# A four-mixer encoder on one core: split weights kept in device memory for a layer's second half, low parts on VectorE, and another clock for the order of emission

## The chip, the cores and the metric

The kernel runs on 1 core of one Trainium2 chip, as one program. The metric is the time of an execution on the device in microseconds (us); less is better. Below, PE is TensorE's matmul, PEld its weight load, DVE is VectorE, ACT ScalarE, POOL GpSimd and SP SyncE; L365 is line 365 of the kernel's file.

## The reference

Input `x` is (1, 1024, 1024) float32: 1024 tokens of 1024 features. Two layers; each normalises its input, projects it once, runs four causal mixers on pieces of the projection, gates and merges them, and adds an output projection. A last normalisation follows.

```python
def _layer(x, norm_w, w_in, ..., w_branch, w_out):
    h = _rmsnorm(x, norm_w)
    p = h @ w_in                                  # 1024 -> 11408 columns
    ...
    u_a = _rwkv7_branch(rw_r, rw_k, rw_v, ...)    # each u is (tokens, 512)
    u_b = _retention_branch(rt_q, rt_k, rt_v, rt_z, ret_norm_w)
    u_c = _ssd_branch(sd_xbc, sd_z, sd_dt, ...)
    u_d = _gdn_branch(gd_qkv, gd_z, gd_b, gd_a, ...)
    gates = jax.nn.sigmoid(gate_logits.reshape(b, s, N_BRANCH, D_MODEL))
    merged = gates[:, :, 0] * (u_a @ w_branch[0])
    ...
    return x + merged @ w_out
```

RWKV-7 and gated DeltaNet are recurrences which the kernel writes chunk by chunk, with the inverse of a unit lower triangular matrix for each chunk and head.

## The kernel before, in words

**Passes.** The 1024 tokens are two halves of 512. A pass is one half of one layer; there are four: layer 0 first half, layer 0 second half, layer 1 first half, layer 1 second half. In the trace they take about 940 us each. A pass has 228 slabs of weights, of 128 x 512 float32 (256 KB); with the output projections of a pass running in the next, all four read 912. The two halves of a layer read the same weights.

**Slabs.** A product takes weights and activations each as a high part H (a cast to the type fp32r) and a low part L = value − H, and sums H·H, H·L and L·H: a slab costs 12 matmuls of 128x512. `prefetch(g)`, when the products get to slab g, has SP load slabs up to g + 5 into `raw` (three buffers), has H made of slabs up to g + 3 (ACT, now and then DVE) and L of those up to g + 2 (`low`, which calls `subtract`), both into `hl` (four buffers). `subtract` is also what makes the L parts of the mixers' outputs (`u`), of the normalised input (`hL`) and of operands inside the units (`w`, `GE`, `GF`). It takes POOL or DVE, by the clock described next.

**What sets the order.** Each engine runs its instructions in the order in which the program was written, so the program's writer matters: `mixers` runs a list of tasks (the steps of 12 units for each pass: 2 retention, 4 DeltaNet, 2 SSD, 4 RWKV-7) and the stream of products, written in `FIRST` and `PLAN`. Whenever a task's next step should be ready by the `Clock`, it is emitted; otherwise a few matmuls of the product stream are. `Clock` is an estimate kept while the program is written: a time for each engine, the last write and read of every 128 elements of a tile, a cost for each kind of instruction, and 0.2 us from engine to engine. `sooner(a, b, n)` asks it which of two engines would be done first. It ends up in no instruction, only in their order.

**Inside a unit.** `inverse` works on `invw`: some twenty small DVE steps on 4 to 128 elements, with small matmuls (`m`) of PE between them. `ev_conv` makes a causal convolution with three DVE instructions on `cvy`. `rsqrt` has POOL take a power into `rs`. SP's queue holds, in the order of writing, the loads of `raw`, the loads of `rope` (two tiles `tg` and `cvy` for each q and k of retention, four pairs a pass), and loads of the next pass's input in `norm`; ACT's queue has the stores of the layer's output and some loads.

Of the kernel before, what the change touches and what calls it, by code (L numbers as in the profile page):

```python
# [16 lines left out]
P = 128  # L17
D = 1024
S = 1024
T = 512          # tokens per pass  # L20
NC = 4           # chunks per pass
C = 128          # tokens per chunk
# [5 lines left out]
# units in the order in which a pass runs them  # L28
# [3 lines left out]
# what a unit takes from the input projection, in the order of the products, with its place in memory; what has two  # L32
# places is 256 columns wide and has the tokens in the partitions
# [11 lines left out]
# The products of a pass in the order in which the tensor engine takes them, between the steps of the units.  # L45
# "out" is the output projection of the pass before, "norm" the normalisation of the input of the next pass;
# the last branch is merged in two steps, gates and projections.
# [4 lines left out]
# the first pass  # L52
# [10 lines left out]
# the others  # L63
# [36 lines left out]
def slabs_of(it):  # L100
    """The slabs of weights of an item of the plan, each of four blocks of 128 rows and 128 columns, or of two of
    128 rows and 256 columns."""
# [16 lines left out]
def sequence(npass):  # L119
    """The items of the plan for all passes, each with its pass."""  # L120
    seq = [(p - (it[0] == "out"), it) for p in range(npass) for it in (PLAN if p else FIRST)]
    return [x for x in seq if x != (npass - 1, ("norm",))] + [(npass - 1, it) for it in PLAN if it[0] == "out"]
# [30 lines left out]
# columns of the packed small parameters  # L153
# [10 lines left out]
def ssd_blk(idx, role):  # L164
    """Index of a 128-wide block of xbc."""
# [46 lines left out]
# constants: name -> (first column, width)  # L212
# [10 lines left out]
def make_consts():  # L223
# [42 lines left out]
    rope = np.stack([ct, st, ct * sc, st * sc])          # 4, P, S  # L266
# [4 lines left out]
class Clock:  # L271
    """An estimate, in microseconds, of when the engines get to what is emitted; it orders the steps."""
    HAND = 0.2       # from one engine to another

    def __init__(self):
        self.t = {e: 0.0 for e in ("pe", "vector", "scalar", "gpsimd", "dma")}
        self.slot, self.owner, self.written, self.read = {}, {}, {}, {}
        self.step = 0.0

    def place(self, tile, key):  # L280
        """The tile lies where the last one with this key lay."""
# [3 lines left out]
    def grains(self, ap):  # L285
        """Pieces of 128 elements of a tile's place which an operand touches; a bank of PSUM counts as one, as its
        users take turns."""
# [12 lines left out]
    def op(self, eng, outs, ins, cost):  # L300
        at = self.t[eng]
        gi, go = [g for a in ins for g in self.grains(a)], [g for a in outs for g in self.grains(a)]
        for g in gi:
            w = self.written.get(g)
            if w:
                at = max(at, w[0] + (0.13 if w[1] == eng else self.HAND))
        for g in go + [g for g in gi if g[1] < 0]:
            for d in (self.written, self.read):
                w = d.get(g)
                if w and w[1] != eng:  # L310
                    at = max(at, w[0] + self.HAND)
        end = self.wait(eng, at) + cost
        for g in gi:
# [10 lines left out]
    def settled(self, *aps):  # L324
        """When the last writes to these operands are over."""
# [6 lines left out]
    def cost(self, eng, name, n):  # L332
        if eng == "vector":
            return 0.07 + n * (0.52e-3 if name == "copy" else 1.04e-3)
        if eng == "scalar":
            return 0.1 + n * 0.83e-3
        return {"memset": 0.1 + n * 0.83e-3, "tensor_copy": 0.2 + n * 3.4e-3, "affine_select": 0.2 + n * 0.85e-3,
                "pow": 0.4 + n * 0.165}.get(name, 0.2 + n * 1.97e-3)


class Engine:
    """An engine whose instructions the clock sees."""
# [4 lines left out]
    def __getattr__(self, what):  # L347
        fn = getattr(self.real, what)

        def call(*a, **k):  # L350
# [8 lines left out]
            else:  # L359
                nm = "pow" if ALU.pow in a else what  # L360
                if what == "tensor_copy" and self.name == "vector" and not any(x.tensor.name.split("_")[0] in "mgy" for x in ops):
                    nm = "copy"
                self.clock.op(self.name, outs, [x for x in ops if not any(x is o for o in outs)],
                              self.clock.cost(self.name, nm, n))
# [11 lines left out]
def finish(gen):  # L376
    """What the generator returns, after all its steps."""
# [12 lines left out]
class Trunk:  # L390
# [12 lines left out]
    # ---------------------------------------------------------------- tiles  # L403
# [29 lines left out]
    # ---------------------------------------------------------------- tensor engine, with its time kept  # L433
    def mm(self, out, lhsT, rhs, **k):
        n, m = (int(np.prod(ap.shape[1:])) for ap in (rhs, lhsT))
        cost = (2 if m > 64 else 1.2) * max(n, m, 16) * 0.84e-3 if rhs.dtype == F32 else max(n, 64) * 0.42e-3
# [1574 lines left out]
```

## Time and profile before

| | |
|---|---|
| median of 3 runs | 3782.73 us (3778.8 to 3783.42) |
| profiled execution, span from first to last instruction | 3775.2 us, 7.5 us below that median; the profile gives no other time of that execution |
| granted TensorE clock | 0.978 |
| busy: PE / DVE / ACT / POOL | 3577.6 / 2543.6 / 1401.4 / 1790.6 us |
| HBM read / written | 280.69 / 10.49 MB |
| loads of `raw` | 912, 256.0 KB each |

A page's matmuls are pipelined and their ends modelled: the busy time of PE counts more than its issue. In lists of groups the columns are: line, engine, operation, out<-in with shapes, count | busy us, mean ns of one | idle time before them and who ended it. In lists of waits: who waits for whom, us in total, times, longest. In windows: stretch, length, then busy us and count for PE, PEld, DVE, ACT, POOL, then granted clock, share of the DMA engines and GB/s.

### The profile page before, as it was taken

What the parts mean: (1) busy time and instruction counts of PE and PEld (TensorE: products, weight loads), DVE (VectorE), ACT (ScalarE), POOL (GpSimd) and SP (SyncE); (2) the same over time, 40 slices, a digit from 0 to 9 for tenths busy, and PEclk for the clock granted to TensorE, in tenths of its full rate; (3) what the DMA queues carried; (4) which work ended last, traced back from release to release, by engine and by line L of the source; (5) the groups of instructions that cost most, each with busy time, mean ns of one, the idle gap of its engine ahead of it and who ended that gap; (6) DMA issues with size and microseconds to landing.
All of it is one profiled execution on the core that took longest, in us unless ns stands there. A gap on an engine that the chain in (4) does not pass through costs nothing. (4 is left out here: it accounts for less than half of the span.)

```text
span 3775.2 us, 66152 instructions
## 1 busy us (share of the span) xinstructions
PE 3577.6 (95%) x24904; PEld 2864.7 (76%) x24904; DVE 2543.6 (67%) x5607; ACT 1401.4 (37%) x3121; POOL 1790.6 (47%) x1846
## 2 busy tenths in 40 slices
PE   7999999999999999999999999999999999999998
PEld 5777877777877787777787778777778778867777
DVE  6678666766577856567657775757665876675664
ACT  4433343333243334333324334433332433443333
POOL 4534554545453445445545445444454534454444
PEclk9999999999999999999999999999999999999999
DMA  3212222113322222212332222221243222221124
GB/s 121 72 59 65 73 72 61 52 60 114 124 76 79 65 73 68 61 54 71 113 126 75 71 73 70 62 64 55 71 125 113 86 64 68 70 65 58 57 76 148
DMA packets 162176, 295.48 MB, mean 78 GB/s; under 512 B 17984, under 2 KB 21440, under 8 KB 161856
## 3 DMA queue, kind: packets, MB, share of 16 engines
q1 hardware_dynamic: 150192, 271.22, 24.1%
q10 hardware_dynamic: 11664, 20.02, 1.6%
q8 instruction: 197, 3.23, 0.4%
q14 instruction: 123, 1.01, 0.1%
HBM read 280.69 MB, written 10.49 MB: 77 GB/s over the span
## 5 line engine op out<-in xcount | busy, mean ns | idle before, releaser
L438 PE MATMUL g<-hH,hl 128*128 128x512 f32 (+1 forms) x5176 | 1773.9, 415 | 8.4 <-DVE cvraw L365 4.9
L365 POOL TENSOR_TENSOR hl<-raw,hl 128x512 fp32r<-128x512 f32 x700 | 960.6, 1377 | 745.0 <-ACT hl L365 659.2
L438 PEld LDWEIGHTS g<-hH,hl 128*128 128x128 f32 (+1 forms) x5176 | 974.9, 191 | 240.5 <-issue 10.3
L438 PE MATMUL g<-hL,hl 128*128 128x512 f32 x2600 | 1040.8, 400 | 0.0
L365 ACT CAST hl<-raw 128x512 fp32r<-128x512 f32 x851 | 521.8, 618 | 684.4 <-PE g L438 270.0
L438 PE MATMUL g<-u,hl 128*128 128x512 f32 (+1 forms) x2112 | 608.9, 411 | 24.1 <-ACT hH L365 9.7
L438 PEld LDWEIGHTS g<-hL,hl 128*128 128x128 f32 x2600 | 496.8, 191 | 113.0 <-issue 8.6
L438 PEld LDWEIGHTS g<-u,hl 128*128 128x128 f32 (+1 forms) x2112 | 391.5, 191 | 122.3 <-ACT hH L365 12.2
L365 POOL TENSOR_TENSOR rs<-rs,mhalf 128x4 f32<-128x4 f32 (+2 forms) x80 | 106.5, 1331 | 401.5 <-DVE rs L365 401.2
L365 DVE SCALAR_TENSOR_TENSOR cvy<-cvraw,par,cvy 128x512 f32<-128x512 f32 x244 | 257.7, 1056 | 41.8 <-ACT cvy L365 30.4
L365 DVE TENSOR_TENSOR hl<-raw,hl 128x512 fp32r<-128x512 f32 x212 | 211.5, 1007 | 27.4 <-ACT hl L365 26.3
L438 PE MATMUL g<-hl,hH 128*128 128x256 f32 x1024 | 190.0, 285 | 2.7 <-DVE hl L365 2.7
L365 DVE TENSOR_TENSOR invw<-invw 128x4 f32<-128x4 f32 (+3 forms) x464 | 164.3, 354 | 15.9
L365 ACT COPY cvraw<-g 128x512 f32<-128x512 f32 (+1 forms) x160 | 93.5, 585 | 187.5 <-PE g L438 145.6
L438 PEld LDWEIGHTS g<-hl,hH 128*128 128x128 f32 x1024 | 160.3, 191 | 3.6 <-DVE hl L365 2.9
L365 POOL TENSOR_SCALAR_AFFINE_SELECT GA<-GA 128x512 f32<-128x512 f32 x128 | 85.2, 672 | 121.8 <-ACT GA L365 121.8
L365 ACT ACTIVATE cvraw<-cvy 128x512 f32<-128x512 f32 x80 | 50.2, 628 | 234.9 <-DVE cvy L365 217.2
L365 POOL TENSOR_TENSOR acc<-acc,tg 128x512 f32<-128x512 f32 x64 | 90.3, 1411 | 81.4 <-DVE tg L365 70.6
L438 PE MATMUL g<-hl,hL 128*128 128x256 f32 x512 | 125.6, 283 | 0.0
L438 PE MATMUL m<-w,w 64*128 64x256 f32 (+1 forms) x640 | 115.5, 312 | 1.3 <-ACT w L365 0.5
L365 ACT ACTIVATE tg<-g 128x512 f32<-128x512 f32 x100 | 59.6, 596 | 150.1 <-PE g L438 109.1
L365 ACT ACTIVATE in<-g 128x512 f32<-128x512 f32 x84 | 49.3, 597 | 169.2 <-PE g L438 169.2
(340 smaller groups left out, 5682.2 us busy)
## 6 DMA issues: line engine op xcount, KB each, us to landing
raw<-W SPq DMA_DIRECT2D x912, 256.0 KB, 2.6
w<-x ACTq DMA_DIRECT2D x32, 256.0 KB, 3.5
tg<-rope SPq DMA_DIRECT2D x16, 256.0 KB, 3.0
cvy<-rope SPq DMA_DIRECT2D x16, 256.0 KB, 3.4
w<-x SPq DMA_DIRECT2D x16, 256.0 KB, 4.4
x<-tg ACTq DMA_DIRECT2D x12, 256.0 KB, 2.1
x<-cvy ACTq DMA_DIRECT2D x12, 256.0 KB, 2.0
GA<-xT SPq DMA_DIRECT2D x8, 256.0 KB, 5.1
```

Of the source, the lines that this page charges most:

```text
L365: return fn(*a, **k)
L438: self.nc.tensor.matmul(out, lhsT, rhs, **k)
```

## The change

Three things change.

**Kept weights.** In a layer's first half (passes of even number) `low` now also stores the finished `hl` tile, H and L together (512 KB), into a tile of device memory, on SP's queue. In the second half no `raw` slab is loaded and nothing is split: `load_slab` loads `hl` from that tile. Such a load is not issued ahead of what `split` was asked for, that is g + 3 in place of g + 5.

**Low parts.** `subtract` always takes DVE.

**Clock.** It has a port that DVE and POOL share: an instruction that `ported` names starts when the port is free and holds it. Several costs are other numbers, matmuls' among them. This changes the order of what is emitted, and what `sooner` answers. Comments went away too.

```diff
 class Clock:
     HAND = 0.2
+    SAME = 0.13
...
+        self.port = 0.0
...
-    def op(self, eng, outs, ins, cost):
+    def op(self, eng, outs, ins, cost, port=False):
...
+        if port:
+            at = max(at, self.port)
         end = self.wait(eng, at) + cost
+        if port:
+            self.port = end
...
-        return {"memset": 0.1 + n * 0.83e-3, "tensor_copy": 0.2 + n * 3.4e-3, "affine_select": 0.2 + n * 0.85e-3,
-                "pow": 0.4 + n * 0.165}.get(name, 0.2 + n * 1.97e-3)
+        return {"memset": 0.1 + n * 0.83e-3, "tensor_copy": 0.13 + n * 1e-3, "affine_select": 0.1 + n * 0.95e-3,
+                "pow": 0.4 + n * 0.15}.get(name, 0.2 + n * 1.97e-3)
+
+    def ported(self, eng, name, ins):
+        if eng == "scalar" or not ins or any(self.slot.get(x.tensor.name, ("",))[0] in ("m", "g", "y") for x in ins):
+            return False
+        return eng == "gpsimd" or name in ("tensor_tensor", "scalar_tensor_tensor", "tensor_copy", "copy") \
+            or (name == "tensor_scalar" and int(np.prod(ins[0].shape[1:])) >= 32)
+
+    def free(self, eng, port=False):
+        return max(self.t[eng], self.port) if port else self.t[eng]
...
-        cost = (2 if m > 64 else 1.2) * max(n, m, 16) * 0.84e-3 if rhs.dtype == F32 else max(n, 64) * 0.42e-3
+        if rhs.dtype != F32:
+            cost = max(n, 128) * 0.456e-3
+        elif m <= 64:
+            cost = 0.03 if m <= 32 else 0.11 if n <= 64 else n * 1.7e-3
+        else:
+            cost = 2 * max(n, m) * 0.85e-3
...
     def split(self, high, low):
         nc = self.nc
+        self.high = high
         flat = lambda ap: ap.rearrange("p k c -> p (k c)")
         for i in range(self.next_low, low + 1):
-            if i in self.hl:
+            if i in self.raw and i in self.hl:
                 self.low(i)
         for i in range(self.slab_next_split, high + 1):
             self.load_slab(i)
+            if self.kept(i):
+                self.slab_next_split = i + 1
+                continue
...
+        p, sl = self.slabs[i]
+        w = self.wsplit[p // NHALF, sl] = self.dr.tile([P, 8 * P], F32, tag=f"ws{i}", name=f"ws{i}")
+        self.nc.sync.dma_start(w, hl.rearrange("p a k c -> p (a k c)").bitcast(F32))
         self.next_low = i + 1
...
     def sooner(self, a, b, n, what=""):
         ck = self.ck
-        return ck.t[a] + ck.cost(a, what, n) <= ck.t[b] + ck.cost(b, what, n) + 0.8
+        at = {e: ck.free(e, e != "scalar") + ck.cost(e, what, n) for e in (a, b)}
+        return at[a] <= at[b] + 0.8

     def subtract(self, out, a, b):
-        e = self.nc.gpsimd if self.sooner("gpsimd", "vector", int(np.prod(out.shape[1:]))) else self.nc.vector
+        e = self.nc.vector
         e.tensor_tensor(out, a, b, ALU.subtract)

     def load_slab(self, i):
         while self.slab_next_dma <= i:
-            r = self.t([P, 4 * P], "raw", bufs=3)
-            self.nc.sync.dma_start(r, self.slab_ap(self.slab_next_dma))
-            self.raw[self.slab_next_dma] = r
+            n = self.slab_next_dma
+            if self.kept(n):
+                if n > self.high:
+                    break
+                p, sl = self.slabs[n]
+                hl = self.t([P, 2, 4, P], "hl", bufs=4, dt=F32R)
+                self.nc.sync.dma_start(hl.rearrange("p a k c -> p (a k c)").bitcast(F32), self.wsplit.pop((p // NHALF, sl)))
+                self.hl[n] = hl
+            else:
+                r = self.t([P, 4 * P], "raw", bufs=3)
+                self.nc.sync.dma_start(r, self.slab_ap(n))
+                self.raw[n] = r
             self.slab_next_dma += 1
+
+    def kept(self, i):
+        return self.slabs[i][0] % NHALF == 1
```

Counted over the whole program: SP's loads of `raw` go from 912 to 456, and 456 stores `ws<-hl` and 456 loads `hl<-ws` join them. POOL's subtractions of slabs go from 700 to 0 and its other subtractions of low parts, 154 of 256 columns and 87 of 512, to 0, DVE's of slabs from 212 to 456; casts of slabs go from 851 to 443 on ACT and from 61 to 13 on DVE. PE has 19362 instructions in both.

SP's queue at the program's start, before (`ws` below is a store into device memory, `raw` a slab's load):

```order
L365 DMA raw_85<-W 128x512
L365 DMA up_87<-up 128x256
L365 DMA raw_159<-W 128x512
L365 DMA raw_163<-W 128x512
L365 DMA raw_165<-W 128x512
L365 DMA raw_178<-W 128x512
```

and with the change:

```order
L387 DMA raw_85<-W 128x512
L387 DMA up_87<-up 128x256
L387 DMA ws_115<-hl_111 128x1024
L387 DMA ws_132<-hl_128 128x1024
L387 DMA ws_163<-hl_160 128x1024
L387 DMA raw_165<-W 128x512
L387 DMA raw_169<-W 128x512
L387 DMA raw_171<-W 128x512
L387 DMA ws_182<-hl_167 128x1024
```

The fourth slab's load, `raw_159` before and `raw_165` now, stands behind the stores of the first three. Further on in a first half stores and loads alternate.

SP's queue where the second pass begins, with the loads for retention's q and k, before:

```order
L365 DMA raw_9159<-W 128x512
L365 DMA raw_9182<-W 128x512
L365 DMA tg_9201<-rope 128x512
L365 DMA cvy_9202<-rope 128x512
L365 DMA raw_9209<-W 128x512
L365 DMA raw_9226<-W 128x512
L365 DMA tg_9247<-rope 128x512
```

and with the change:

```order
L387 DMA ws_9529<-hl_9507 128x1024
L387 DMA ws_9552<-hl_9531 128x1024
L387 DMA hl_9554<-ws_163 128x1024
L387 DMA hl_9574<-ws_182 128x1024
L387 DMA hl_9594<-ws_203 128x1024
L387 DMA tg_9613<-rope 128x512
L387 DMA cvy_9614<-rope 128x512
L387 DMA hl_9618<-ws_241 128x1024
L387 DMA hl_9632<-ws_295 128x1024
L387 DMA tg_9653<-rope 128x512
```

The first kept slabs come right behind the last stores, and the two `rope` loads stand among loads of `hl` where they stood among loads of `raw`.

DVE's queue in the third pass, at the start of the inverse of an RWKV-7 unit that the prediction shows at 2529.88 us (`invw` is the inverse's work tile, `GR` what its first small matmuls take, `hl<-raw` a slab's low part), before:

```order
L365 SCALAR_TENSOR_TENSOR GD_22_24801<-in_36_23388,par_17647,w_31_24006 128x2x128
L365 TENSOR_TENSOR GD_22_24801<-in_36_23448,w_31_24006 128x2x128
L365 TENSOR_TENSOR GF_31_24808<-w_43_24228,GF_31_24808 128x256
L365 TENSOR_TENSOR GE_31_24807<-GD_22_24801,w_59_24806 128x512
L365 TENSOR_TENSOR invw_16_24817<-GA_23_24651,con_81 32x128 x4
L365 TENSOR_REDUCE invw_16_24817<-invw_16_24817 128x32
L365 TENSOR_TENSOR GR_22_24652<-invw_16_24817,con_81 128x64
L365 TENSOR_TENSOR GR_22_24652<-invw_16_24817,con_81 128x32
L365 TENSOR_TENSOR GR_22_24652<-invw_16_24817,con_81 128x16
L365 COPY invw_16_24817<-con_81 128x32
L365 TENSOR_SCALAR sh_24827<-strw_1_92,em_24014 128x128
L365 TENSOR_TENSOR invw_16_24817<-m_24868,invw_16_24817 128x4
```

and with the change:

```order
L387 TENSOR_TENSOR hl_24816<-raw_24725,hl_24816 128x512
L387 SCALAR_TENSOR_TENSOR GD_22_24891<-in_36_23390,par_17491,w_31_24115 128x2x128
L387 TENSOR_TENSOR GD_22_24891<-in_36_23456,w_31_24115 128x2x128
L387 TENSOR_TENSOR w_63_24894<-w_53_24282,w_63_24894 128x256
L387 TENSOR_TENSOR w_50_24895<-w_39_24287,w_50_24895 128x256
L387 TENSOR_TENSOR GF_31_24898<-w_43_24289,GF_31_24898 128x256
L387 TENSOR_TENSOR GE_31_24897<-GD_22_24891,w_59_24896 128x512
L387 TENSOR_TENSOR invw_16_24907<-GA_23_24735,con_81 32x128 x4
L387 TENSOR_REDUCE invw_16_24907<-invw_16_24907 128x32
L387 TENSOR_TENSOR GR_22_24736<-invw_16_24907,con_81 128x64
L387 TENSOR_TENSOR GR_22_24736<-invw_16_24907,con_81 128x32
L387 TENSOR_TENSOR GR_22_24736<-invw_16_24907,con_81 128x16
```

DVE now has a slab's low part and two of the unit's (`w`) ahead of the inverse's first steps; the steps themselves stand in the same order. Three rows further on another slab's low part, `hl_24877<-raw_24770`, comes ahead of the inverse's next step.

More of the change, by code (lines that the diff above doesn't have):

```diff
@@ L305, in op @@
             if w:
-                at = max(at, w[0] + (0.13 if w[1] == eng else self.HAND))
+                at = max(at, w[0] + (self.SAME if w[1] == eng else self.HAND))
         for g in go + [g for g in gi if g[1] < 0]:
@@ L362, in call @@
                     nm = "copy"
-                self.clock.op(self.name, outs, [x for x in ops if not any(x is o for o in outs)],
-                              self.clock.cost(self.name, nm, n))
+                ins = [x for x in ops if not any(x is o for o in outs)]
+                c, port = self.clock.cost(self.name, nm, n), self.clock.ported(self.name, what, ins)
+                if port and what == "scalar_tensor_tensor":
+                    c += n * 0.12e-3
+                if self.name == "scalar" and k.get("accum_out") is not None:
+                    c += 0.15
+                self.clock.op(self.name, outs, ins, c, port)
             return fn(*a, **k)
@@ L440, in tr @@
     def tr(self, out, in_, ident):
-        self.ck.op("pe", [out], [in_], max(out.shape[-1], in_.shape[-1]) * 0.84e-3)
+        self.ck.op("pe", [out], [in_], max(out.shape[-1], in_.shape[-1]) * 0.86e-3)
         self.nc.tensor.transpose(out, in_, ident)
@@ L453, in setup @@
         self.slab_pos = 0
+        self.wsplit = {}
         self.units_done = 0
```

## The prediction

> **What bounds the kernel now.** I read the page first, then who TensorE waits for, then one of those waits in the timeline, then the DMA share of the stretches where TensorE runs densest.
>
> ```profile
> span 3775.2 us, 66152 instructions
> PE 3577.6 (95%) x24904; PEld 2864.7 (76%) x24904; DVE 2543.6 (67%) x5607; ACT 1401.4 (37%) x3121; POOL 1790.6 (47%) x1846
> ```
>
> PE is the bound: 95% busy, 197.6 us idle (3775.2 − 3577.6). No other engine is near full, so a change can win only what PE waits, plus what its modelled ends hide. The chain that ended last shows how much they hide: in the last dense stretch 324 products take 75.27 us, 0.232 us each, while the page gives the same kind 0.414 us.
>
> ```profile
> 3685.14 75.27 PE g L438 x324
> L438 PE MATMUL g<-hH,hl 128*128 128x512 f32 x5152 | 1762.0, 414 | 8.4 <-DVE cvraw L365 4.9 <-DVE hl L365 2.0 <-POOL hl L365 1.3
> ```
>
> So a wait seen as idle time is about 0.18 us (0.414 − 0.232) longer than it shows. Whom PE waits for:
>
> ```profile
> PE m L438 <- DVE invw L365: 77.3, 62, 2.7
> PE m L438 <- DVE GR L365: 13.8, 10, 3.6
> PE m L438 <- DVE GE L365: 12.9, 18, 1.5
> PE m L438 <- DVE stgdn L365: 11.0, 14, 1.9
> ...
> PE m L438 <- DVE b L365: 0.2, 1, 0.2
> ```
>
> These are the first four and the last of 16 rows that name DVE; together they are 161.2 us in 149 waits. With 149 × 0.18 = 27 us hidden, PE loses about **188 us** to DVE. All other releasers (ACT hH, ACT u, POOL hl and so on) are about 24 us. Why DVE is late is seen at one of the longest waits, in the third pass, at 2531 us (start, length, engine, instruction):
>
> ```profile
> 2528.18 1.77 DVE L365 TENSOR_TENSOR GE<-GD,w 128x512 fp32r<-128x512 f32 x1
> 2529.37 1.72 POOL L365 TENSOR_TENSOR hl<-raw,hl 128x512 fp32r<-128x512 f32 x1
> 2529.88 2.61 DVE L365 TENSOR_TENSOR invw<-GA,con 32x128 f32<-32x128 f32 x4
> 2532.94 1.48 DVE L365 TENSOR_TENSOR GR<-invw,con 128x64 f32<-128x64 f32 x3
> 2534.56 0.74 PE L438 MATMUL m<-GR,con 128*128 128x112 f32 x2 [2.68 <-DVE invw L365]
> ...
> L365 DVE TENSOR_TENSOR invw<-GA,con x128: 268/289/1362, 562.5 to 3636.5; 32x128 f32<-32x128 f32 x128
> L365 DVE TENSOR_TENSOR invw<-invw x464: 166/168/1349, 198.4 to 3644.8; 128x4 f32<-128x4 f32 x87, 128x8 f32<-128x8 f32 x41, 128x16 f32<-128x16 f32 x23, 128x32 f32<-128x32 f32 x4
> L365 DVE TENSOR_TENSOR hl<-raw,hl x212: 655/698/1790, 20.3 to 3718.8; 128x512 fp32r<-128x512 f32 x106
> ```
>
> The last three rows give min/median/max in ns. Four small products of `invw` take 2.61 us, though one takes 0.289 in the median (1.16 for four); they begin while POOL subtracts a low part until 2531.09, and the next such row stretches too. DVE instructions that read two SBUF tiles stop while POOL works, up to about 1.3 us each. That lateness, 1.45 us here alone, is most of PE's 2.68.
>
> **The change, part by part.** *POOL's low parts go to DVE.* The order counts 700 subtractions of slabs less on POOL, 154 of 256 columns and 87 of 512.
>
> ```profile
> L365 POOL TENSOR_TENSOR hl<-raw,hl 128x512 fp32r<-128x512 f32 x700 | 960.6, 1377 | 745.0 <-ACT hl L365 659.2 <-DVE hl L365 52.7 <-PE m L438 16.6
> L365 POOL TENSOR_TENSOR w<-w,w 128x256 fp32r<-128x256 f32 x56 | 46.4, 847 | 21.1 <-ACT w L365 21.1
> L365 POOL TENSOR_TENSOR u<-yC,u 128x512 fp32r<-128x512 f32 x30 | 44.0, 1466 | 16.9 <-ACT u L365 16.9
> ```
>
> POOL loses 960.6 + 154 × 0.847 + 87 × 1.466 = 1219 us of 1790.6, that is 68%; 572 us stay. I take PE's waits on DVE to shrink in the same proportion, since what makes DVE late is being stopped by POOL: 188 × 0.68 = **−128 us**. Bounds: nothing gained (DVE late for its own queue's sake), and all 188.
>
> *What DVE gets.* Slab subtractions go from 212 to 456: 244 × 0.698 = 170 us. The 154 narrow ones, at an estimated 0.40 (a little over half of 0.698), are 62, the 87 wide ones 61. Casts fall from 61 to 13:
>
> ```profile
> L365 DVE CAST hl<-raw 128x512 fp32r<-128x512 f32 x61 | 40.3, 661 | 75.9 <-PE g L438 58.1 <-DMA raw<-W 14.2 <-POOL hl L365 3.5
> L365 DVE SCALAR_TENSOR_TENSOR cvy<-cvraw,par,cvy 128x512 f32<-128x512 f32 x244 | 257.7, 1056 | 41.8 <-ACT cvy L365 30.4
> L365 DVE SCALAR_TENSOR_TENSOR cvy<-cvraw,par,cvy x244: 750/752/1710, 138.0 to 3243.6; 128x512 f32<-128x512 f32 x122
> L365 DVE TENSOR_TENSOR hl<-raw,hl 128x512 fp32r<-128x512 f32 x212 | 211.5, 1007 | 27.4 <-ACT hl L365 26.3
> L365 DVE TENSOR_TENSOR invw<-invw 128x4 f32<-128x4 f32 (+3 forms) x464 | 164.3, 354 | 15.9
> ```
>
> 48 × 0.661 = 32 less, so +261 gross. What comes back is mean less median: 244 × 0.304 for `cvy`, 212 × 0.309 for `hl`, 464 × 0.186 for `invw`: 226 us in three groups, of which 68% is 154, and the groups below them give more. DVE ends near 2543.6 + 261 − 154 = 2650, at most 70% of the span. I cost this at nothing: PE's products hide it, and in the second halves DVE loses its slab work altogether. If that cover is gone, the price is the slower rival below.
>
> *ACT* loses 408 casts (851 to 443), 250 us of an engine that is 37% busy: nothing.
>
> *The stores and the double loads.* 456 raw loads stay, 456 stores and 456 loads of 512 KB join, all on SP's queue. In a first half each slab then moves 768 KB (786 kB) where it moved 256; the two halves differ only there.
>
> ```profile
> 975.00:1000.00 25.00, 25.00 (x156) 22.11 (x155) 11.22 (x21) 7.50 (x13) 11.42 (x9) 1.00 0.46 141
> 3685.00:3760.00 75.00, 75.00 (x325) 60.57 (x324) 39.24 (x52) 27.69 (x46) 32.55 (x24) 1.00 0.48 155
> raw<-W SPq DMA_DIRECT2D x912, 256.0 KB, 2.6
> x<-tg ACTq DMA_DIRECT2D x12, 256.0 KB, 2.1
> SPq L365 <- DVE in L365: 36.8, 12, 8.1
> ```
>
> The last two columns of the windows are the share of the DMA engines and GB/s: a full share would carry 141/0.46 = 307 to 155/0.48 = 323 GB/s. A slab of 12 products takes PE 12 × 0.232 = 2.79 us at its densest, the 786 kB 2.43 to 2.56. It fits, barely; a store of 256 KB lands in 2.1 us, no slower than a load. Value 0; upper bound, should stores and loads mixed run a fifth slower: 3.2 us, 0.4 us a slab over the (496 + 540)/12 = 86 slabs of the two 100 us stretches around the ends of the first halves, **+35**.
>
> ```profile
> 900.00:1000.00 100.00, 96.51 (x496) 79.70 (x495) 63.69 (x89) 36.71 (x63) 55.79 (x38) 0.98 0.43 132
> 2800.00:2900.00 100.00, 99.89 (x540) 82.31 (x539) 56.64 (x109) 30.64 (x59) 43.15 (x31) 1.00 0.42 132
> ```
>
> The Trainium skill (SBUF — State Buffer, the summary of rules for kernel authors) counts 358 GB/s between HBM and SBUF, which would make a slab 2.2 us; the trace's share implies less, and I keep the trace's. By either figure the term is zero.
>
> In a second half a slab's load takes the place of the slab four before it, so it is issued when PE ends that one, three slabs (8.4 us) ahead of its use. It lands in an estimated 2.6 + 0.85 (262 kB more at 307) = 3.5 us. Queued ahead of it on SP stand, eight times in the two second halves, a pair of `rope` loads that wait for their tiles: the row above has SP waiting 3.1 us in the mean and 8.1 at most for DVE's `in`. The slack of 4.9 is then sometimes overrun: 1 us a time, **+8**; the loads of the next pass's input (`norm`) and the crossing from one half to the other, +7. At the start the fourth raw load now stands behind the stores of slabs 0 to 2, hence behind their low parts: +3. Together **+18**, bounds 0 and 60.
>
> *The emission clock.* It moves steps between products but adds no work: PE has the same 19362 instructions. Value 0; bounds −60 (the rest of the 188) and +128 (new misfits give the gain back).
>
> Sum: 3775.2 − 128 + 18 = 3665 for the profiled span. The median of the three runs shown, 3782.7, lies 7.5 above that span, so the forecast for a median is **3673 us**, 2.9% below.
>
> **Rivals.**
> A, *nearly all the waits go*: an order that fits the engines takes the other 60 us as well. For it: in the next pass the same four steps take the same 2.61 us, so such waits come from a fixed order that another can avoid.
>
> ```profile
> 3458.27 2.61 DVE L365 TENSOR_TENSOR invw<-GA,con 32x128 f32<-32x128 f32 x4
> ```
>
> Against: pieces such as PE → DVE → PE round trips stay. 3673 − 60 = 3613.
> B, *the waits move*: DVE's queue, now with the subtractions of `u`, `hL` and `w` in it, is late at other steps, and half or more of the gain is lost: −128 becomes −50, so 3751. For it: in a first half DVE has to make a low part every slab between steps of the inverse. And the stop may be mutual: a subtraction on DVE would hold up the POOL steps that stay, the powers of `rs` above all, for which DVE waits in turn.
>
> ```profile
> L365 POOL TENSOR_TENSOR rs<-rs,mhalf 128x4 f32<-128x4 f32 (+2 forms) x80 | 106.5, 1331 | 401.5 <-DVE rs L365 401.2
> ```
>
> 80 × 0.698 = 56 us at most of such lateness, inside B's price of 78. The Trainium skill (SBUF — State Buffer, § Who interferes with whom) has it so: the port that VectorE and GpSimd share is held for the whole instruction, and whichever starts second waits. By that rule the trace of 2529.88 is explained, and the stop would also run this other way. Against B: 0.698 is short beside what POOL's stops cost.
> C, *slower: DVE becomes the bound of the first halves.* One mechanism: if DVE is stopped by something other than POOL's subtractions, nothing comes back, and a first half (here the first pass) gets 228 − 53 low parts, half the narrow and wide ones, and few casts less.
>
> ```profile
> 0.00:940.00 940.00, 877.15 (x6100) 699.08 (x6101) 642.70 (x1412) 359.01 (x810) 453.26 (x472) 0.97 0.25 74
> ```
>
> 642.7 + 175 × 0.698 + 62 − 6 = 821 us of 940: DVE's idle falls from 297 to 119 us. With less than half of it left I let the first halves' part of PE's waits (94 of 188) double: 3775 + 94 + 18 + 7.5 = 3895. It decides from the point where DVE passes about 80% of a first half. Against: the minimum of 166 ns beside the mean of 354 for one small instruction; such a spread is a stop, and POOL's 1.3 us fits its maximum.
> D, *the loads are late*: DMA binds in the dense stretches and SP's queue holds back loads in the second halves, +35 and +60 in place of +18: 3673 + 77 = 3750. For it: 786 kB against 2.79 us leaves a tenth. Against: the dense stretches are short.
> E, *no change*: POOL's stops go, but PE waits as long for DVE's longer queue, 3775 to 3790.
>
> **How the numbers follow.** Forecast (3630 to 3715) 0.52; A 0.14; B 0.12; D 0.07; E 0.06; C 0.09. About 0.2% (7.6 us) is what a measurement of this kernel can tell from no change. A, the forecast, and nearly all of B and D are faster: 0.85. Of E most is within the bound: 0.05. Slower: C and a little of E: 0.10. For 8 in 10 the range reaches from A's centre, 3610, to the upper edge of B and D, 3770; C and E and the lower half of A lie outside. The likeliest one's own range is 3630 to 3715.
>
> **What would show it.** Right: `hl` gone from POOL, POOL near 570 us; DVE's `invw<-invw` at a mean under 220 ns and `cvy` under 850; the row "PE m <- DVE invw" under 40 us, PE idle under 120; in the second halves no row of PE waiting for a DMA `hl<-ws` beyond some 10 us in all; landings of that load near 3.5 us; a DMA share in the dense stretch of the first pass between 0.8 and 1. Wrong: DVE over 80% in 0 to 940 with PE waiting for it as before (C); PE waiting in first place for ACT `hl` or DMA `raw` (D); small `invw` rows still beyond 300 ns, which would mean that POOL's subtractions were not what stops DVE.

## The result, and the profile after

The change takes 3681.69 us (median; 3674.63 to 3689.41), the kernel before on the same chip 3783.07 us (3778.8 to 3791.84). The ratio is **0.9725, 95% interval 0.9702 to 0.9747**: 2.7% faster. The forecast was 3673. The execution profiled below was the longest of its kernel, 3689.41 us, 1.7 above its span.

The page of the change, the span and the engines:

```profile
span 3687.7 us, 65225 instructions
PE 3557.8 (96%) x24904; PEld 2858.0 (78%) x24904; DVE 2296.0 (62%) x6041; ACT 1182.9 (32%) x2711; POOL 580.3 (16%) x905
```

POOL lost 1210.3 us, which is what the diff takes from it. DVE took over 485 subtractions (244 of slabs, 154 narrow, 87 wide) and lost 48 casts, and still fell by 247.6 us. PE's idle time fell from 197.6 to 129.9 us.

Its groups of instructions, first those that the prediction named on DVE, then the costliest that stay on POOL:

```profile
L387 DVE TENSOR_TENSOR hl<-raw,hl 128x512 fp32r<-128x512 f32 x456 | 334.1, 738 | 61.0 <-ACT hl L387 59.9
L387 DVE SCALAR_TENSOR_TENSOR cvy<-cvraw,par,cvy 128x512 f32<-128x512 f32 x244 | 187.1, 767 | 77.1 <-ACT cvy L387 68.4 <-ACT carrw L387 0.5
L387 DVE TENSOR_TENSOR invw<-invw 128x4 f32<-128x4 f32 (+3 forms) x464 | 88.4, 191 | 15.9
L387 POOL TENSOR_TENSOR rs<-rs,mhalf 128x4 f32<-128x4 f32 (+2 forms) x80 | 106.3, 1328 | 1055.4 <-DVE rs L387 1055.3
L387 POOL TENSOR_TENSOR acc<-acc,tg 128x512 f32<-128x512 f32 x64 | 90.0, 1407 | 202.9 <-DVE tg L387 167.9 <-PE m L465 13.8 <-DVE invw L387 13.0
L387 POOL TENSOR_SCALAR_AFFINE_SELECT GA<-GA 128x512 f32<-128x512 f32 x128 | 85.5, 676 | 225.5 <-ACT GA L387 205.9 <-DVE invw L387 19.4
L387 POOL COPY GR<-invw 32x128 f32<-32x128 f32 x192 | 64.5, 336 | 236.8 <-DVE invw L387 230.6
```

The same DVE groups by tile, min/median/max in ns:

```profile
L387 DVE TENSOR_TENSOR hl<-raw,hl x456: 649/685/1786, 4.7 to 2958.6; 128x512 fp32r<-128x512 f32 x152
L387 DVE SCALAR_TENSOR_TENSOR cvy<-cvraw,par,cvy x244: 750/752/1483, 136.6 to 3179.3; 128x512 f32<-128x512 f32 x122
L387 DVE TENSOR_TENSOR invw<-invw x464: 166/168/1284, 202.7 to 3553.6; 128x4 f32<-128x4 f32 x87, 128x8 f32<-128x8 f32 x41, 128x16 f32<-128x16 f32 x23, 128x32 f32<-128x32 f32 x4
```

The medians are those of before (for `hl` 685 in place of 698); the means have come down towards them: `cvy` from 1056 to 767 over a median of 752, `invw<-invw` from 354 to 191 over 168, `hl` from 1007 to 738 over 685. The stops have not gone altogether, as the maxima show. Of the steps in the same inverse, those with one input in `m`, which lies in PSUM (the memory that matmuls write), were not long before and did not change; before, and with the change:

```profile
L365 DVE TENSOR_TENSOR invw<-m,invw 128x4 f32<-128x4 f32 (+3 forms) x480 | 86.9, 181 | 21.3 <-PE m L438 6.8
L387 DVE TENSOR_TENSOR invw<-m,invw 128x4 f32<-128x4 f32 (+3 forms) x480 | 87.2, 182 | 18.1 <-PE m L465 3.6
```

The prediction named only steps that read two SBUF tiles. That is too narrow: the copies `cvraw<-carcv`, which read one, fell from 739 to 177 ns in the mean of 40, and `w<-in,con`, which scales one tile by a constant for each partition, from 454 to 279 in 128.

Whom PE waits for now (us in total, times, longest):

```profile
PE m L465 <- DVE invw L387: 20.5, 24, 3.6
PE g L465 <- DVE hl L387: 17.5, 20, 3.1
PE g L465 <- DMA hl<-ws: 16.0, 9, 4.1
PE g L465 <- DVE cvraw L387: 11.0, 7, 4.1
PE m L465 <- DVE w L387: 10.7, 4, 4.6
...
PE g L465 <- DVE cvy L387: 5.4, 3, 2.1
...
PE m L465 <- DVE GE L387: 1.6, 4, 0.5
PE m L465 <- DVE GR L387: 1.4, 2, 0.7
```

`invw` fell from 77.3 to 20.5, `GE` and `GR` from 12.9 and 13.8 to almost nothing. Longer are the waits for low parts (`hl` from 4.7 to 17.5, `w` from 4.2 to 10.7) and for work queued beside them on DVE; new are those for the kept weights. All rows that name DVE are 85.5 us in 75 waits, from 161.2 in 149.

The stretches of 920 us from the start, of which the first is most of pass 1 and the second most of pass 2 (the last two columns are the share of the DMA engines and GB/s):

```profile
0.00:920.00 920.00, 864.27 (x6054) 690.19 (x6055) 646.66 (x1629) 361.15 (x808) 155.95 (x238) 0.97 0.57 196
920.00:1840.00 920.00, 906.97 (x6362) 731.79 (x6361) 514.96 (x1415) 243.05 (x571) 141.47 (x222) 0.98 0.46 155
```

DVE is 70% busy in a first half, far from a bound. The new transfers and the loads of `raw`, from issue to landing:

```profile
ws<-hl SPq DMA_DIRECT2D x456, 512.0 KB, 3.2
hl<-ws SPq DMA_DIRECT2D x456, 512.0 KB, 3.3
raw<-W SPq DMA_DIRECT2D x456, 256.0 KB, 3.8
```

The kept slab lands in 3.3 us, but `raw`, between the stores, now in 3.8 where it took 2.6.

### The profile page after: what moved, and what is told of

Read it like the earlier page. It is cut to its first block, busy times and chain, and to the rows that moved or that the text cites. A ratio compares the mean times of both kernels' runs of the same rounds, so it can differ in the third digit from the quotient of the medians.

```text
span 3687.7 us, 65225 instructions
## 1 busy us (share of the span) xinstructions
PE 3557.8 (96%) x24904; PEld 2858.0 (78%) x24904; DVE 2296.0 (62%) x6041; ACT 1182.9 (32%) x2711; POOL 580.3 (16%) x905
## 4 chain that ended last, share of the span: by engine, by line
PE 78%; DVE 13%; DMA 5%; issue 2%; ACT 2%; POOL 1%; SPq 0%; DVEq 0%; ACTq 0%
PE g L465 56%; PE m L465 16%; DVE invw L387 4%; PE m L469 3%; PE y L465 3%; DMA raw<-W 2%; DVE hl L387 1%; DMA hl<-ws 1%; DVE w L387 1%; DVE cvy L387 1%; DVE in L387 1%; ACT cvraw L387 1%; DVE hL L387 1%; DMA w<-rd 0%; DMA w<-x 0%
## 5 line engine op out<-in xcount | busy, mean ns | idle before, releaser
L465 PEld LDWEIGHTS g<-hH,hl 128*128 128x128 f32 (+1 forms) x5176 | 963.9, 190 | 255.4 <-issue 22.0
L465 PE MATMUL g<-u,hl 128*128 128x512 f32 (+1 forms) x2112 | 610.2, 413 | 34.3 <-DVE hl L387 10.7
L387 ACT CAST hl<-raw 128x512 fp32r<-128x512 f32 x443 | 273.8, 620 | 493.7 <-DMA raw<-W 232.5
L387 DVE TENSOR_TENSOR hl<-raw,hl 128x512 fp32r<-128x512 f32 x456 | 334.1, 738 | 61.0 <-ACT hl L387 59.9
L387 POOL TENSOR_TENSOR rs<-rs,mhalf 128x4 f32<-128x4 f32 (+2 forms) x80 | 106.3, 1328 | 1055.4 <-DVE rs L387 1055.3
L387 DVE SCALAR_TENSOR_TENSOR cvy<-cvraw,par,cvy 128x512 f32<-128x512 f32 x244 | 187.1, 767 | 77.1 <-ACT cvy L387 68.4
L387 POOL TENSOR_SCALAR_AFFINE_SELECT GA<-GA 128x512 f32<-128x512 f32 x128 | 85.5, 676 | 225.5 <-ACT GA L387 205.9
L465 PEld LDWEIGHTS m<-w,w 64*128 64x128 f32 (+1 forms) x640 | 86.9, 195 | 25.6 <-issue 12.1
L387 POOL COPY GR<-invw 32x128 f32<-32x128 f32 x192 | 64.5, 336 | 236.8 <-DVE invw L387 230.6
L465 PEld LDWEIGHTS g<-hl,hL 128*128 128x128 f32 x512 | 99.0, 193 | 3.3 <-DVE hL L387 2.6
```

The lines of the kernel that those rows point to most:

```text
L387: return fn(*a, **k)
L465: self.nc.tensor.matmul(out, lhsT, rhs, **k)
```

## The experiments

Three parts can be taken one by one: K, the kept weights; V, low parts always on VectorE; C, the new clock. Six kernels are the other combinations. In these the helper's line is L393 and the matmul's L473.

**V alone.** From before:

```diff
     def subtract(self, out, a, b):
-        e = self.nc.gpsimd if self.sooner("gpsimd", "vector", int(np.prod(out.shape[1:]))) else self.nc.vector
+        e = self.nc.vector
```

> Only the low parts go to VectorE; weights are split in all four passes and the emission clock is that of before. DVE gets 912 slab subtractions instead of 212, POOL none. Theory (POOL's subtractions stop DVE, and PE waits for the stopped DVE): POOL near 570 us, DVE near 2600 to 2700 us, PE's waits on DVE down by about half, ratio to before 0.975 to 0.987. Rival 'the order does it': the old clock does not fit the new placement, ratio 0.995 to 1.01. Rival 'kept weights do it' (less splitting is the gain): DVE is only fuller, ratio 1.00 to 1.02.

3700.79 us, ratio 0.9769 (0.9741 to 0.9797). One line gives 2.3 of the change's 2.75%. Here DVE makes all low parts of all four passes, and is busier than before (2605.7 us) by only 62, so most of its added work came back from the stops. PE's waits for DVE, though, fall by a quarter only (161.2 to 121.7 us), where half was expected.

**K alone.** From before, `low` stores the finished slab and `load_slab` loads it in the second half, as in the change; `subtract` and `Clock` are left as before:

```diff
     def low(self, i):
...
+        w = self.wsplit[p // NHALF, sl] = self.dr.tile([P, 8 * P], F32, tag=f"ws{i}", name=f"ws{i}")
+        self.nc.sync.dma_start(w, hl.rearrange("p a k c -> p (a k c)").bitcast(F32))
         self.next_low = i + 1
```

> Only the kept weights: second halves load H and L from device memory; the low parts go to POOL or DVE by the old clock. POOL's slab subtractions fall from 700 to about 360, DVE's from 212 to 98. Theory: POOL loses about 470 us of port time, 39% of the 1219, so about 0.39 of the gain, 40 us, ratio 0.985 to 0.993, with the gain in the second halves. Rival 'kept weights do it': ratio 0.970 to 0.980. Rival 'the order does it': 0.995 to 1.005.

3725.33 us, ratio 0.9828 (0.98 to 0.9856). The engines, from its page:

```profile
PE 3560.7 (96%) x24904; PEld 2855.1 (77%) x24904; DVE 2244.8 (60%) x5446; ACT 1164.0 (31%) x2693; POOL 1309.2 (35%) x1519
```

The gain is larger than the theory had it (0.985 to 0.993) and smaller than the first rival. POOL loses 481 us here too, since half of the slabs are no longer split, and PE's waits for DVE fall to 118.5 us. K alone thus seems to work in part by the same means as V: 1.7 and 2.3% alone, where a product of the two ratios would be 0.960, and K and V together, below, give 0.971.

**C alone.** From before, the whole new `Clock` and `sooner`, and nothing else:

```diff
     def sooner(self, a, b, n, what=""):
         ck = self.ck
-        return ck.t[a] + ck.cost(a, what, n) <= ck.t[b] + ck.cost(b, what, n) + 0.8
+        at = {e: ck.free(e, e != "scalar") + ck.cost(e, what, n) for e in (a, b)}
+        return at[a] <= at[b] + 0.8
```

> Only the emission clock; asked which engine is done sooner it now gives POOL 856 of the 912 slab subtractions, and nearly all others. Theory: POOL gets fuller, 1950 to 2150 us, DVE is stopped as often or more, ratio 0.99 to 1.015. Rival 'the order does it': PE's waits on DVE fall by half, ratio 0.970 to 0.985.

3948.59 us, ratio **1.0424** (1.0397 to 1.0452): slower, and by more than either expectation. Its group of slab subtractions on POOL:

```profile
L393 POOL TENSOR_TENSOR hl<-raw,hl 128x512 fp32r<-128x512 f32 x856 | 1151.7, 1355 | 644.2 <-ACT hl L393 580.1 <-issue 37.9 <-DMA raw<-W 12.0
```

The new estimate has one port for both engines, so when the port comes free last, both engines are taken to start at the same time; POOL's longer cost (0.2 + 512 × 1.97e-3 = 1.21 us, DVE's 0.07 + 512 × 1.04e-3 = 0.60) is then within the 0.8 us that `sooner` allows it, and POOL is named: 856 of 912 slabs go there, where 700 went before. PE's waits for DVE rise from 161.2 to 223.2 us, but also those for POOL itself, from 3.6 to 42.7: here work on POOL is late in its own right too. The count alone does not give the price, for 156 slabs more cost more than taking all 700 away gains. Whether `sooner` is the way by which C loses is told by the next three.

**K and V, without C.** From the change:

```diff
     def ported(self, eng, name, ins):
+        return False
```

and the former costs and `sooner` in place of the new.

> Kept weights and low parts on VectorE, with the emission clock of before. Theory: most of the gain is here without the new clock, ratio 0.973 to 0.985, PE's waits on DVE under 100 us. Rival 'the order does it': ratio 0.99 or more.

3679.78 us, ratio 0.9712 (0.9688 to 0.9736), a little better than expected and beside 0.9725 for the change.

**V and C, without K.** From the change:

```diff
-        w = self.wsplit[p // NHALF, sl] = self.dr.tile([P, 8 * P], F32, tag=f"ws{i}", name=f"ws{i}")
-        self.nc.sync.dma_start(w, hl.rearrange("p a k c -> p (a k c)").bitcast(F32))
...
     def kept(self, i):
-        return self.slabs[i][0] % NHALF == 1
+        return False
```

> Low parts on VectorE and the new emission clock, without kept weights. The clock alone was slower (1.042). Theory a: it was slower because it put 856 of 912 slab subtractions on POOL, whose steps stop DVE; with them on VectorE nothing of that is left, ratio 0.972 to 0.982, like low parts alone (0.977). Theory b: its order itself is worse; the factors multiply, 0.977 x 1.042 = 1.018, and more than 1.00 in any case.

3701.89 us, ratio 0.9758 (0.9725 to 0.9791), beside 0.9769 without C.

**K and C, without V.** From the change, `subtract` asks `sooner` again:

```diff
     def subtract(self, out, a, b):
-        e = self.nc.vector
+        e = self.nc.gpsimd if self.sooner("gpsimd", "vector", int(np.prod(out.shape[1:]))) else self.nc.vector
```

> Kept weights and the new clock, low parts where the clock says: 427 slab subtractions on POOL, 29 on DVE. Theory a (the clock's harm comes by POOL's subtractions): POOL 1350 to 1500 us, ratio 0.985 to 1.005, slower than kept weights alone (0.983) by half of the clock's 4.2% at most. Theory b (the order itself): 0.983 x 1.042 = 1.024.

3783.2 us, ratio 0.998 (0.9965 to 0.9996), beside 0.9828 without C. POOL makes 427 of the 456 low parts of slabs.

So C costs 4.2% and 1.5% where `subtract` asks the clock, and nothing that can be measured (0.9712 to 0.9725, 0.9769 to 0.9758) where it does not. With V the order of emission that it makes is neither better nor worse. What hurts comes only where its answer to `sooner` places the low parts, and V takes that question away; whether the new order, too, fits a POOL with low parts badly is not separated. K is worth some 0.6% on top of V without C, and 0.3% with C, where the intervals overlap.

**What on POOL stops DVE.** Two kernels give POOL idle work of about the same length, three or six instructions before each slab's products, whose result nothing reads. One kind reads two constants from SBUF, the other only writes. From the change:

```diff
         self.prefetch(g)
+        for x in range(3):
+            a = self.con[:, 128 * x:128 * x + 128]
+            self.tc.nc.gpsimd.tensor_tensor(self.scr, a, a, ALU.subtract)
         return self.hl.pop(g)
```

> The changed kernel with three idle subtractions of 128x128 on POOL at every slab (2736, reading constants into a spare tile that nobody uses); every other engine has the same instructions in the same order. POOL goes from 580 to about 1700 us. Theory (POOL steps that read stop DVE): DVE rises from 2296 towards 2550 us, invw<-invw rises from 0.20 us towards 0.30, PE's waits on DVE return, ratio to before 0.982 to 1.00. Rival (the work moved off POOL mattered through its own lateness, not through the stop): ratio stays at 0.970 to 0.976, DVE within 2% of 2296.

3759.58 us, ratio 0.9916 (0.9887 to 0.9944): 1.9 of the 2.75% are lost again. Its engines, and groups of its instructions:

```profile
PE 3570.8 (95%) x24904; PEld 2860.8 (76%) x24904; DVE 2432.0 (65%) x6041; ACT 1181.9 (31%) x2711; POOL 1891.4 (50%) x3641
```

```profile
L640 POOL TENSOR_TENSOR scr<-con 128x128 bf16<-128x128 f32 x2736 | 1327.3, 485 | 188.8
L393 DVE TENSOR_TENSOR hl<-raw,hl 128x512 fp32r<-128x512 f32 x456 | 357.2, 789 | 61.9 <-ACT hl L393 60.8
L393 DVE TENSOR_TENSOR invw<-invw 128x4 f32<-128x4 f32 (+3 forms) x464 | 99.8, 215 | 15.9
```

DVE runs the same 6041 instructions, in the same order, in 136 us more. PE waits longer for it, 140.7 us in 123 waits over all rows; the first two:

```profile
PE m L473 <- DVE invw L393: 35.0, 43, 3.6
PE g L473 <- DVE hl L393: 28.7, 20, 3.9
```

With memsets in place of the subtractions:

```diff
         self.prefetch(g)
+        for _ in range(6):
+            self.tc.nc.gpsimd.memset(self.scr, 0.0)
         return self.hl.pop(g)
```

> As the run before, but with six idle memsets of 128x128 at every slab (5472): POOL writes and reads nothing, for about as long, 1.1 ms more. If only POOL steps that read stop DVE: ratio 0.970 to 0.977, DVE within 2% of 2296 us. If any POOL step stops DVE: like the run before, 0.982 to 1.00.

3680.27 us, ratio 0.971 (0.9683 to 0.9737): nothing lost. Its engines, and the group of the memsets:

```profile
PE 3538.9 (96%) x24904; PEld 2844.8 (77%) x24904; DVE 2292.2 (62%) x6041; ACT 1183.1 (32%) x2711; POOL 1682.0 (46%) x6377
```

```profile
L639 POOL MEMSET scr<- 128x128 bf16 x5472 | 1127.3, 206 | 296.1
```

POOL is nearly as busy as before the change, and DVE as short as after it; PE waits 96.0 us for DVE. So it is not a busy POOL that delays DVE but a POOL that reads. A memset is also shorter than a subtraction, 206 ns against 485. An estimate of what that could do: if a stop lasted for what is left of POOL's instruction, the sum of squares (5472 × 206² against 2736 × 485², 0.36) would leave 49 of the 136 us; DVE shows −4. Writing is not wholly free: `w<-in,con`, 279 ns in the change, takes 307 beside the memsets (333 beside the subtractions), 3.6 us in all. The Trainium skill (SBUF — State Buffer, § Who interferes with whom) says that a DVE instruction with two SBUF inputs contends with a GpSimd instruction that reads SBUF and not with one that only writes it; by that rule the two kernels come out as they did, 2432.0 and 2292.2 us on DVE.

**Room on the DMA queue.** Each kept slab is stored a second time, into a tile that nothing reads:

```diff
         self.nc.sync.dma_start(w, hl.rearrange("p a k c -> p (a k c)").bitcast(F32))
+        w2 = self.dr.tile([P, 8 * P], F32, tag=f"wt{i}", name=f"wt{i}")
+        self.tc.nc.sync.dma_start(w2, hl.rearrange("p a k c -> p (a k c)").bitcast(F32))
```

> The changed kernel with every finished slab stored twice (the second copy is read by nobody): 456 stores of 512 KB more, so a first half's slab moves 1280 KB where the change moves 768. Same order on every other engine. If the DMA of the change is hidden with room to spare (prediction's value 0): the first halves near a DMA share of 0.9, ratio to before 0.973 to 0.985. If it is at its limit already (rival D): 120 MB more a first half at 350 GB/s are 340 us each, ratio 1.05 or more.

3835.38 us, ratio 1.0129 (1.0094 to 1.0164), between the two expectations. The first stretch of its windows, and its transfers:

```profile
0.00:920.00 920.00, 839.75 (x5909) 669.36 (x5910) 614.09 (x1574) 344.94 (x782) 155.61 (x237) 0.96 0.81 300
```

```profile
ws<-hl SPq DMA_DIRECT2D x456, 512.0 KB, 4.5
wt<-hl SPq DMA_DIRECT2D x456, 512.0 KB, 5.0
raw<-W SPq DMA_DIRECT2D x456, 256.0 KB, 5.3
```

The second store brings the share in the first half from 0.57 to 0.81 and `raw`'s landing from 3.8 to 5.3 us, and costs 4% of the time: about 150 us, long before the share is 1. ACT, which casts the slabs, waits 461.5 us for `raw` where it waited 232.5 in the change, and 17.7 us for stores to give back an `hl` buffer: so it is the late loads, and hardly the buffers that the stores hold. One set of stores fits, but it stands ahead of the loads of `raw`, and there is no room for a second. That suggests taking them out of the loads' way:

```diff
     def prefetch(self, g):
...
         self.load_slab(min(g + 5, tot - 1))
+        self.stores()
...
-        self.nc.sync.dma_start(w, hl.rearrange("p a k c -> p (a k c)").bitcast(F32))
+        self.tostore.append((w, hl))
```

> The changed kernel with the stores of finished slabs put behind the next load on SP's queue instead of ahead of it; PE, DVE, ACT and POOL have the same order. The trace of the change shows SP standing 7.5 and 12.5 us in stores that wait for DVE's low parts where a first half ends, the first kept loads behind them, and PE waiting 4.5, 3.1 and 4.5 us for these. Theory (the loads are late because of SP's order): landing of raw falls from 3.8 to about 3 us, PE's waits for hl<-ws from 16 to under 8 us, ratio to before 0.967 to 0.971. Rival (they are late because PE frees the buffer late): 0.971 to 0.974, waits for hl<-ws as before.

3663.3 us, ratio 0.9676 (0.9647 to 0.9706), so about 0.5% better than the change, with intervals that just overlap. `raw` lands in 3.2 us in place of 3.8, the store in 4.1 in place of 3.2. The longest waits for kept loads in the change are 4.1, 2.7 and 4.1 us, a little less than the expectation has them. At the same places 1.9, 0 and 0.8 us are left; but one of 2.9 us has come at 1783 us, and PE's wait for the kept slabs did not fall as far as expected:

```profile
PE g L473 <- DMA hl<-ws: 10.8, 10, 2.9
```

**Fewer steps that read, on POOL.** Every `tensor_tensor` of POOL but the powers goes to DVE (`acc`, `sf` and the like, 269 instructions):

```diff
         def call(*a, **k):
+            if self.name == "gpsimd" and what == "tensor_tensor" and ALU.pow not in a:
+                return self.peer.tensor_tensor(*a, **k)
```

> The changed kernel with all that is left of POOL's tensor_tensor steps (300 or so, the powers excepted) on DVE too. POOL falls from 580 to about 330 us. Theory taken to its end: DVE's remaining stops, about 80 us, halve; DVE gets about 130 us of work; ratio to before 0.966 to 0.973. Rival (DVE's own queue now weighs more than the stops): 0.973 to 0.985.

3650.56 us, ratio 0.9641 (0.9613 to 0.9669), faster than the change and than the theory's 0.966 to 0.973. The order of emission changes with this edit; a new order by itself, C beside V, moved the time by little over 0.1%. Here the lines are L395 and L476. Its engines, two groups, and PE's wait for `invw`:

```profile
PE 3537.5 (97%) x24904; PEld 2841.4 (78%) x24904; DVE 2352.9 (64%) x6310; ACT 1179.9 (32%) x2711; POOL 329.8 (9%) x635
```

```profile
L395 DVE TENSOR_TENSOR hl<-raw,hl 128x512 fp32r<-128x512 f32 x456 | 311.8, 690 | 65.8 <-ACT hl L395 65.0
L395 DVE TENSOR_TENSOR invw<-invw 128x4 f32<-128x4 f32 (+3 forms) x464 | 82.6, 178 | 16.0
```

```profile
PE m L476 <- DVE invw L395: 9.2, 15, 2.8
```

To take over 250.5 us of POOL's work makes DVE only 56.9 us longer. The mean of `hl` is now within 5 ns of the 685 that was its median, and the wait for `invw` is less than half of what the change left.

**Both at once**, the stores behind the loads and the `tensor_tensor` steps on DVE:

> The change with both edits at once: a pass's stores of kept slabs stand behind the loads on SP's queue, and of the three-operand steps only the powers stay on POOL. Theory (the two act on different waits, the one on PE's waits for loads and on the order, the other on DVE's stops): the gains add, 0.9641 less about 0.005 that the stores' place gave, so a ratio of 0.956 to 0.962, with POOL near 330 us and PE's waits for hl<-ws near 11 us. Rival (each only removed some gaps of PE that the other removes too, or both are within what a new order of emission gives by chance): a ratio of 0.963 to 0.968.

3637.3 us, ratio **0.9602** (0.9588 to 0.9615): the gains add, and this is the fastest kernel of the study, 1.2% below the change. Its page and its clock:

```profile
span 3635.6 us, 65091 instructions
PE 3529.9 (97%) x24904; PEld 2837.2 (78%) x24904; DVE 2353.3 (65%) x6310; ACT 1180.9 (32%) x2711; POOL 331.5 (9%) x635
```

```profile
core 0: 3635.6 us, clock 0.988
```

Its waits for `hl<-ws` are 7.6 us where 11 were expected.

## Why the prediction was right, and where its steps were not

**Forecast and mechanism.** The time (3681.69 against 3673) lies in the likeliest case's own range, 3630 to 3715. POOL's subtractions stop DVE, and DVE's lateness is most of what PE waits for: V alone, the reads on POOL and the writes on POOL show the two halves of that. POOL at 580.3 (572 forecast), `invw<-invw` at 191 ns (under 220), `cvy` at 767 (under 850), PE's wait for `invw` at 20.5 (under 40) and the landing at 3.3 (3.5) came as written.

**The main term, −128, was mis-sized.** PE's loss to DVE goes from 188 to 85.5 + 75 × 0.18 = 99 us: **−89**. Two errors partly cancel. First, the share. I took POOL's whole 1790.6 us as what stops DVE, so that 1219 was 68%. The memsets show that steps which read nothing do not count, and moving the other three-operand steps away (250.5 us) took most of what was left of the stops. Against those alone 1219 is 1219/(1219 + 250.5) = 83% (the powers, copies and selects that stay on POOL read too; no run separates them); and the four rows that I take to have been long because of stops (`invw`, `GR`, `GE`, `stgdn`) did fall from 115.0 to 23.5, by 80%. Second, I let the same share fall off every wait for DVE, and put nothing for the work that joins its queue. `hl`, `w`, `cvraw` (the products' row), `cvy` and `hL` went from 13.8 to 47.0 us. That is rival B's mechanism, worth 33 us; B priced it at 78. The other half of B, powers of `rs` held up by DVE's subtractions, does not show: their mean is 1328 ns, 1331 before.

**DVE near 2650 was wrong: 2296.0.** The gross addition, +261, holds: a slab's subtraction takes 685 ns in the median (0.698 in the sum), and the narrow ones of `w` 0.42 (0.40). What came back is 2543.6 + 261 − 2296.0 = 509 us, where the sum had 154. The three groups that I counted gave 194: `cvy` 257.7 − 187.1 = 71, `invw` 164.3 − 88.4 = 76, `hl` 211.5 + 170 − 334.1 = 47. The other 315 came from the other groups, which I named and then left at zero. It did no harm to the time, because DVE is not the bound; a right figure would have left C, which rests on a full DVE, less of a chance.

**Loads, +18: right in size, in part by luck.** PE waits 16.0 us in 9 waits for `hl<-ws`, 17.6 with what is hidden. The row to look for was "beyond some 10 us", so by that sign the loads were later than the forecast said, and by the sum they were as late. But 10.9 us are three waits (at 916, 2027 and 2746 us) for kept loads behind stores that wait for DVE's low parts, as SP's queue shows ahead of the first:

```profile
903.57 7.53 SPq L387 DMA_DIRECT2D ws<-hl  x3
911.20 1.72 SPq L387 DMA_DIRECT2D hl<-ws  x3
```

The sum had 7 for the crossings and the next pass's input together. Its 8 for `rope` shows as two waits of 0.8 and 0.7 us behind such loads, and its 3 for the start not at all: PE is busy 44.6 of the first 60 us, 41.9 before.

**Stores, 0: right only as far as it goes.** The DMA share in the dense stretch was put between 0.8 and 1. Of the first pass's stretches of 50 us in which PE is never idle, the one with the highest share:

```profile
500.00:550.00 50.00, 50.00 (x242) 39.98 (x241) 35.44 (x75) 25.27 (x59) 7.18 (x12) 1.00 0.67 237
```

0.67 here and 0.57 over the pass. I had taken PE's densest rate, one product in 0.232 us, for all of a dense stretch; here 171 of the 242 matmuls are of slabs and the others are the mixers', so a slab takes 50 × 12/171 = 3.5 us in place of 2.79. The reason given, that it fits in bandwidth, was the lesser one. What matters is the place in SP's queue: a second store costs 4% at a share of 0.81, and standing behind the loads brings 0.5%.

**The clock, 0: right for the change and for the wrong reason.** I argued that it only moves steps. It also answers `sooner`, and where that places the low parts C costs 1.5 to 4.2%; I did not follow that the same diff's `subtract` no longer asks.

**PE's idle, under 120: missed** at 129.9, by the 33 us of moved waits less what fell further than forecast.

**The sum again, against the profiled spans.** DVE's waits −89; kept slabs +17.6; other releasers from 23.8 us in 24 waits to 17.0 in 9, −9.5; and the granted clock, next section, −6. That is −87, and the spans differ by 3687.7 − 3775.2 = −87.5; the clock's figures have three digits, good for some 2 us each, so the closer agreement is luck. The clock's part was not in my sum at all, and it is smaller here than between other executions: the profiled execution of before is a short one, that of the change the longest of its four, with a clock of 0.979 where the others have 0.982 to 0.984. Between the spans the sum of −110 misses by 22; that the medians, 101 us apart, came within 9 us of the forecast is in part luck. Of the rivals, A (3613) did not come with this change, but the fastest kernel above, with most of the reading steps off POOL, is more than half of the way from the forecast to it; C, D and E fell.

## What the runs showed of the hardware that I had not expected

**After a pause of PE of 2 us the clock often falls to half.** In before, PE waits at 570 us for `invw` (timeline, and windows around it; the clock is the third column from the right):

```profile
569.71 1.09 PE L438 MATMUL g<-hH,hl 128*128 128x512 f32 x4
573.01 0.45 PE L438 MATMUL m<-invw,GA 32*32 32x32 f32 x32 [2.21 <-DVE invw L365]
```

```profile
568.00:573.00 5.00, 2.80 (x13) 1.89 (x12) 4.35 (x16) 1.93 (x5) 3.92 (x6) 1.00 0.29 60
573.00:577.00 4.00, 3.99 (x75) 3.48 (x76) 1.92 (x7) 2.03 (x4) 0.85 (x2) 0.57 0.15 58
```

PE is idle 2.21 us, and then, fully busy again, has a granted clock of 0.57 for 4 us. The trace's record of the clock has this as a stretch of 3.4 us at half speed from 573.5; of the 382 such stretches in the 14 profiles of this study 368 last a whole multiple of 3.41 us, mostly one to three. Over the same profiles I counted the pauses of PE by length, and after how many the clock fell to half during the pause or within 4 us after it: of those from 0.3 to 1 us 77 of 706, from 1 to 1.5 us 42 of 195, from 1.5 to 2 us 55 of 130, from 2 to 2.5 us 74 of 101, from 2.5 to 4 us 148 of 181, over 4 us 68 of 73. Pauses that lie close together are counted each, so this is an association and no run here varies the length of one pause alone. The Trainium skill (TensorE: Matmul & The Clock Gate, Part 1: The HAM clock gate) has the half rate set in after at least one idle window of about 3.4 us; here shorter pauses are followed by it more often than not from about 2 us up, and the measurement decides.

What this costs is at most the span times what the clock lacks of 1; for a part of the slow time PE is idle anyway. Before and the clock alone:

```profile
core 0: 3775.2 us, clock 0.978
```

```profile
core 0: 3952.8 us, clock 0.953
```

3775.2 × 0.022 = 83 us before; 3952.8 × 0.047 = 186 with the clock alone, so up to 103 of its 178 us of longer span go with the slower clock and not with the waits as such (74, from 72 to 146, when only the time in which PE is busy is counted). The change, at 0.979, has 77 us, and the fastest kernel, at 0.988, 44 (68 and 35 by PE's busy time). Of the 52 us between these two spans 33 are the clock's by either count. The same idle time is therefore likely to be dearer as a few long waits than as many short ones.

**The place in the queue weighs as much as the size.** 512 KB of `hl`, with few stores beside them, land in 3.3 us where 256 KB of `raw`, among the stores, take 3.8; without stores, before, those took 2.6.

## What to carry to other kernels

Where short VectorE instructions have a mean far above their median, look at what GpSimd reads at that time, not at how busy it is: 1127 us of memsets cost nothing and 1327 us of small subtractions cost 1.9%. When work is moved to the engine that was being stopped, count the stops over all its groups and not over the largest three, and put a price on the waits for the work that joins its queue. When several edits come together, ask of each whether another has taken away the question that it answers: here the new clock is 4.2% slower alone, 1.5% slower beside the kept weights, and without effect once low parts no longer ask it.
